# Window attention in a diffusion backbone: full-height low keys with zeros, masks added on VectorE with the row maximum, rotation by shifted multiplications

## Chip, cores and metric

One Trainium2 chip, of which the program uses one core. The metric is the device time of one execution in microseconds. The engines are named as in the profile: PE (TensorE matmul), PEld (its weight load), DVE (VectorE), ACT (ScalarE), POOL (GpSimd) and SP (SyncE, which here issues the DMAs).

## What is computed

A backbone of two layers runs over 256 context tokens and 256 latent tokens of width 1024. Layer 0 is feed-forward, DeltaNet, feed-forward; layer 1 is feed-forward, window attention, feed-forward. Of layer 1's attention only the latent outputs count. The part of the reference that matters here, cut down:

```python
q = _rms_norm(q.reshape(n_batch, n, SWA_HEADS, SWA_HEAD_DIM), q_gain)      # 16 heads of 64
k = _rms_norm(k.reshape(n_batch, n, SWA_KV_HEADS, SWA_HEAD_DIM), k_gain)   # 4 key heads
if rotate:                                       # latent tokens only
    q, k = _rope(q, cos, sin), _rope(k, cos, sin)
...
allowed = (jnp.abs(t_pos[:, None] - s_pos[None, :]) <= WINDOW) & (s_pos >= 0) & (s_pos < n_tok)
s_ctx = jnp.einsum('bqhgd,bkhd->bhgqk', qb, kc).astype(jnp.float32)
s_win = jnp.where(allowed, jnp.einsum('bqhgd,bkhd->bhgqk', qb, kb).astype(jnp.float32), -jnp.inf)
p = _sink_softmax(jnp.concatenate([s_ctx, s_win], axis=-1), sink_hg).astype(vb.dtype)
return (jnp.einsum('bhgqk,bkhd->bqhgd', p[..., :ctx_len], vc)
        + jnp.einsum('bhgqk,bkhd->bqhgd', p[..., ctx_len:], vb))
```

`_rope` splits the 64 features of a head in halves x1, x2 and gives x1 cos - x2 sin and x1 sin + x2 cos. The softmax has one more logit per head, the sink.

## The kernel before

Features lie on partitions: tokens are kept as 8 chunks of [128 features, 512 tokens], of which columns 0 to 255 are context (`CTX`) and 256 to 511 latent (`LAT`). Every product with a weight is made in three passes of a reduced fp32 format (fp32r): high times high, high times low, low times high (`mm3`). Weights are streamed from memory in tiles `raw` and `ub`; `_split` (L428) cuts them in high parts (a copy on ACT) and low parts (a subtraction, on DVE, or on POOL while `lo_pool` is set, as during the query projections). `w_ahead` (L458) keeps up to four units of 128 output columns split ahead of use. Working tiles [128, 512] come from a pool `u` of 76, PSUM tiles `mm` from its 8 banks. All other engines' instructions have the line L180 in the profile, matrix products L276, transposes L281, since a helper records them.

The order of work is set while the program is written out, by a class `Sched` (L65). It keeps a clock of TensorE work. Straight-line code advances it; background generators say how long they expect to wait (`self.at(...)`) and are resumed when the clock gets there. `note` (L93) estimates when an instruction of another engine ends from its engine and its width. So an instruction that is added, or dropped, moves the others in every engine's queue; each engine then works through its own queue in order.

The attention, `attention` (L1800), goes so:

- Its constants (`att_consts`, L1668) are loaded during the feed-forward block ahead of it: the rotation matrix `rotm`, a block matrix `blk64` for the norms, cosines and sines, the gains, the sinks, and `wmask`, [128, 384], made of three 128-column masks by ACT copies.
- Four units are projected first: two key units (two heads each) and two value units. Then the queries, eight pairs of heads `u`, one unit each.
- `att_qk` (L1691) works on a pair of heads. ACT squares, PE sums the squares over each head (`blk64`), ACT makes the inverse root with Ln and Exp, DVE multiplies by gain and root (`kn`). For latent tokens PE multiplies by `rotm` (L1706), which swaps the halves of a head and gives one the minus sign; DVE multiplies this product, in PSUM, by the sines; POOL multiplies `kn` by the cosines and adds. Then ACT copies the high parts and DVE subtracts for the low ones. A query tile holds the high part of one head in 64 partitions and its low part in the other 64; a key tile holds the high part twice; the keys' low parts of both heads share one tile.
- `att_worker` (L1740): four workers take 16 tasks, a pair of heads `u` by a tile of 128 latent queries `qt`. For each of the two heads, scores over 512 keys are three products into one PSUM bank: query (high and low) by high keys, 128 rows deep; identity by mask, 256 columns (L1755); high query by low keys, 64 rows deep (L1756). DVE takes the row maximum from PSUM (L1760), two small DVE operations bring in the sink, ACT makes the exponential from PSUM with the sum (L1767), DVE scales the rows, PE transposes them in four pieces, ACT copies, PE multiplies by the values, ACT and DVE write the high and low parts of the output.
- Behind the queries `begin` and `out_blocks` make the output projection, whose first products can stand among the attention's.

The lines of the scores before:

```python
rw = slice(64 * par, 64 * par + 64)
sc.append(self.cht())
self.mm(sc[par], q[par][:, qs], kh[par], stop=False)
self.mm(sc[par][:, LAT], self.identr, self.wmask[:, 128 - 128 * qt:384 - 128 * qt], start=False, stop=False)
self.mm(sc[par], q[par][rw, qs], kl[rw, :], start=False)
```

Of the kernel before, what the change touches and what calls it, by code (L numbers as in the profile page):

```python
# [22 lines left out]
def constants():  # L23
    """Arrays that depend on shapes alone."""
    c = {"ident": np.eye(128, dtype=np.float32)}
    # 128 rows: two chunks of 64 tokens; in variant e the half e runs forward and the other one backward
# [20 lines left out]
    d = np.arange(64)  # L47
    for b in (0, 64):
        at[b + 32 + np.arange(32), b + np.arange(32)] = -1.0
        at[b + np.arange(32), b + 32 + np.arange(32)] = 1.0  # L50
        at[b:b + 64, 128 + b:192 + b] = 1.0 / 64
# [8 lines left out]
    at[:, 768:1024] = np.sin(ang.astype(np.float64)).T[f]  # L60
    c["atc"] = at
    return c


class Sched:  # L65
    """Emission order: straight-line code advances a clock of TensorE work, and
    background generators are resumed when the clock reaches the time they asked for."""
# [9 lines left out]
    @staticmethod  # L77
    def cells(a):
        """a tile in parts of 64 partitions by 128 columns"""
        (ps, n), *rest = a.ap  # L80
        p, lo = divmod(a.offset, ps)
        hi = lo + sum((k - 1) * st for st, k in rest)
        return [(a.tensor.name, i, j) for i in range(p // 64, (p + n - 1) // 64 + 1)
                for j in range(lo // 128, hi // 128 + 1)]
# [8 lines left out]
    def note(self, eng, ins, outs, n, extra):  # L93
        """estimates when an instruction of another engine ends"""
# [14 lines left out]
    def product(self, ins, out, ns):  # L109
        """TensorE at the clock, other work first while the operands are awaited"""  # L110
# [59 lines left out]
class Queue:  # L170
    """an engine whose instructions are also noted in the schedule"""
# [38 lines left out]
class Kernel:  # L210
# [34 lines left out]
    def at(self, *aps):  # L245
        """time from now until these are expected"""
        return max(0.0, self.s.when(*aps) - self.s.clock)

# [35 lines left out]
    def mm3(self, ps, w, h, nk, sl=ALL, ks=None, start=True, stop=True):  # L284
        """ps[:, sl] = W^T h over nk chunks of 128, W and h in exact high and low parts."""
# [12 lines left out]
    def plan_weights(self):  # L298
        """Raw loads and the units of 128 output columns cut from them, in the order of use."""
# [4 lines left out]
        def raw(*parts):  # L304
            # outside of DeltaNet its tiles take loads as well
# [11 lines left out]
        def cols(mat, r0, nk, c0, w=256):  # L317
            """nk chunks of 128 rows from r0, w columns from c0 -> [128, nk, w]"""
# [91 lines left out]
    def _load(self, late=False):  # L410
        """loads into the raw tiles that are free, or soon (late = True: any that have no further use)"""
# [46 lines left out]
    def w_ahead(self):  # L458
        """splits the units to come once their loads are expected"""
# [29 lines left out]
    def setup(self):  # L489
# [18 lines left out]
        # tokens  # L508
# [6 lines left out]
        # modulation of the first norm and the first pairs of the first FFN, 128 features after the other  # L515
# [3 lines left out]
        # squares and transposes of the tokens  # L519
# [16 lines left out]
        # root mean squares of the tokens, from tokens on partitions to a row for every partition  # L536
# [12 lines left out]
    def setup_rows(self, rows):  # L549
        """vectors with their features on partitions"""  # L550
# [25 lines left out]
    def first_load(self, c):  # L576
        """weights of the first modulation and of the first pairs of the first FFN for 128 features"""
# [20 lines left out]
    def first_mod(self, c):  # L598
        """shift and scale of (layer 0, slot 0) for 128 features, and their norm"""
# [41 lines left out]
    def first_w(self, c):  # L641
        """high and low parts of the weights of 128 features"""
# [109 lines left out]
    def sq_block(self, d, sl, ps=None):  # L752
        """adds the squares of chunk d to the running sum"""
# [38 lines left out]
    def h_chunks(self, hf, l, slot, ks, pace=None):  # L792
        """high and low parts of the modulated norm of chunks ks, one group of tokens"""
# [70 lines left out]
    def mm_narrow(self, ps, w, sl):  # L864
        """W^T H for 32 columns in two parts: the high and the low part of W with the high part of H, and the high part
        and zeros with the low one"""
# [6 lines left out]
    def halves_first(self, n, evac, narrow=False):  # L873
        """the first n units, context tokens before latent ones"""
# [20 lines left out]
    def out_block(self, d, final):  # L895
        """the latent tokens of chunk d, tokens on partitions, to the output"""
# [15 lines left out]
    def out_blocks(self, h, nk, sl, l, v, nxt, final=None, begun=None):  # L912
        """X += gate * (W^T h); with nxt the squares of the sums and the next norm follow"""
# [77 lines left out]
    def start_pairs(self):  # L991
        """the first three pairs of the first FFN, chunk by chunk as the modulation arrives"""
# [19 lines left out]
    # Tokens of each segment are kept in the order of chunks 0, 3, 1, 2, so that 128 columns q hold the two chunks  # L1012
    # that the forward and the backward pass visit in the same step.
    # kinds of projection: 0 q, 1 k, 2 v, 3 z
# [38 lines left out]
    def dn_gates(self, ps):  # L1053
        """per-token gates from the projection in two parts of [32, 512], tokens on partitions, for both variants"""
# [58 lines left out]
    def dn_unit(self, kind, h, ps):  # L1113
        """evacuates the projection of head h: kind 0 q, 1 k, 2 v, 3 z"""
# [55 lines left out]
    def dn_ss(self, sq, g, dst):  # L1170
        """log of the sums of squares over the head dimension, tokens on partitions"""
# [14 lines left out]
    def dn_pairs(self, ps, lhs, rhs, g, qp):  # L1186
        """products over the head dimension inside each chunk, for two pairs of chunks and four heads"""
# [8 lines left out]
    def dn_prep(self, g):  # L1196
        """decays, the systems of each chunk and their inverses for the heads of group g"""
# [703 lines left out]
```

## Time and profile before

| | |
|---|---|
| runs | 1937.22, 1942.4 and 1944.46 us, median 1942.4 |
| profiled execution | span 1937.3 us; no time of its own beside the span is listed |
| busy in the span | PE 97%, PEld 81%, DVE 66%, ACT 49%, POOL 34% |
| first key norm on DVE | 1601.3 us |
| first row maximum | 1625.3 us |
| end of the last subtraction of the attention | 1714.7 us |
| row maxima, 32 | 21.0 us of DVE |
| mask products, 32 | 8.9 us of PE by the records |

How to read it: times in the trace are counted from the span's start. A group names output and inputs by the program's tiles without their numbers (`mm` is a PSUM bank, `u` a working tile, `st` a small tile of row statistics), then the shape. "Idle before" is the idle time of that engine right ahead of the instruction, with what ended it. Matmul records overlap by some ns, since their ends are modelled; how often one recurs says more than its length. PEclk is the granted TensorE clock as a share of full speed.

### The profile page before, as it was taken

The page shows a single profiled execution, that of the slowest core. Times are in us where ns is not written, and L with a number is a line of the kernel's source. Part 1 is how long each engine was busy: PE and PEld are TensorE (multiplying, and loading weights), DVE is VectorE, ACT ScalarE, POOL GpSimd, SP SyncE. Part 2 cuts the span into 40 slices and gives each one's busy share as a digit, 9 for nine tenths or more (in the row PEclk, how much of TensorE's full clock was granted, in tenths as well). Part 3 has the DMA queues.
Part 4 walks back from the last instruction along what each step waited for, and adds up shares of the span by engine and source line. Part 5 has one row for each costly group of instructions (what it writes and reads, how often), then busy time and mean ns, then how long its engine had stood idle before and what let it go on. Part 6 is the DMA issues. An engine that isn't in the chain of part 4 may idle for free.

```text
span 1937.3 us, 30131 instructions
## 1 busy us (share of the span) xinstructions
PE 1880.2 (97%) x11367; PEld 1560.9 (81%) x11367; DVE 1280.2 (66%) x2065; ACT 946.5 (49%) x2061; POOL 649.8 (34%) x597
## 2 busy tenths in 40 slices
PE   7999999989999999999999999999999999999999
PEld 5878788887776766887888888888888898689998
DVE  4897878855977966578888555643343356856565
ACT  4544544556476555464454344542222357755442
POOL 3344534454546435354445114320000057230000
PEclk8999999999999999999999999999999999999999
DMA  9655454413232152445645554433232334125552
GB/s 292 212 202 203 165 185 169 157 44 126 71 88 81 51 186 82 169 142 185 211 170 179 190 185 147 164 124 101 96 109 87 100 86 96 36 66 174 196 175 87
DMA packets 242376, 270.78 MB, mean 140 GB/s; under 512 B 11015, under 2 KB 198687, under 8 KB 242231
## 3 DMA queue, kind: packets, MB, share of 16 engines
q1 hardware_dynamic: 241943, 268.69, 42.4%
q8 instruction: 89, 1.46, 0.3%
q14 instruction: 56, 0.46, 0.1%
q0 software_dynamic: 144, 0.11, 0.0%
q10 hardware_dynamic: 144, 0.07, 0.0%
HBM read 258.34 MB, written 10.49 MB: 139 GB/s over the span
## 4 chain that ended last, share of the span: by engine, by line
PE 57%; DVE 6%; ACT 3%; issue 3%; POOL 1%; DMA 1%; POOLq 0%; DVEq 0%; ACTq 0%; SPq 0%
PE mm L276 56%; DVE u L180 5%; ACT u L180 3%; PE mm L281 1%; POOL u L180 1%; DVE st L180 1%; DVE big L180 0%; DMA u<-ZD 0%; DMA u<-XD 0%; DVE ub L180 0%; ACT L180 0%; POOLq L180 0%; DVEq L180 0%; ACT sc L180 0%; ACTq L180 0%
## 5 line engine op out<-in xcount | busy, mean ns | idle before, releaser
L276 PE MATMUL mm<-u 128*128 128x512 f32 (+6 forms) x10112 | 1798.5, 343 | 21.3 <-ACT u L180 9.6
L276 PEld LDWEIGHTS mm<-u 128*128 128x128 f32 (+2 forms) x10112 | 1491.4, 185 | 305.9 <-issue 54.4
L180 POOL TENSOR_TENSOR u<-u 128x512 f32<-128x512 f32 (+4 forms) x389 | 430.3, 1112 | 911.4 <-ACT u L180 868.3
L180 ACT ACTIVATE u<-u 128x256 f32<-128x256 f32 (+8 forms) x335 | 159.6, 488 | 488.1 <-DVE u L180 475.8
L180 ACT ACTIVATE u<-mm 128x512 f32<-128x512 f32 (+3 forms) x356 | 142.5, 414 | 283.1 <-PE mm L276 213.8
L180 DVE TENSOR_TENSOR u<-raw,u 128x512 fp32r<-128x512 f32 (+2 forms) x272 | 217.9, 845 | 27.3 <-ACT u L180 26.0
L180 DVE SCALAR_TENSOR_TENSOR u<-u,cc 128x512 f32<-128x512 f32 x196 | 229.3, 1170 | 3.9 <-DMA u<-in_ada_w 0.6
L180 DVE TENSOR_TENSOR u<-ub,u 128x512 fp32r<-128x512 f32 x254 | 199.8, 830 | 18.5 <-ACT u L180 17.3
L180 ACT ACTIVATE u<-raw 128x512 fp32r<-128x512 f32 (+1 forms) x374 | 205.8, 604 | 10.8 <-PE mm L276 5.7
L180 ACT ACTIVATE u<-u,cc 128x512 f32<-128x512 f32 x224 | 151.9, 711 | 82.5 <-DMA u<-in_ada_w 72.4
L180 DVE TENSOR_TENSOR u<-u,mm 128x512 f32<-128x512 f32 (+1 forms) x88 | 54.5, 619 | 206.5 <-PE mm L276 198.2
L180 POOL TENSOR_TENSOR u<-raw,u 128x512 fp32r<-128x512 f32 x98 | 130.4, 1354 | 135.7 <-ACT u L180 119.1
L180 ACT ACTIVATE u<-ub 128x512 fp32r<-128x512 f32 (+1 forms) x284 | 156.0, 605 | 10.2 <-DMA ub<-in_ffn_w 6.0
L180 DVE SCALAR_TENSOR_TENSOR u<-mm,mod,u 128x256 f32<-128x256 f32 x192 | 86.1, 478 | 106.4 <-PE mm L276 106.2
L180 DVE TENSOR_TENSOR u<-u 128x512 fp32r<-128x512 f32 (+5 forms) x125 | 82.6, 662 | 74.3 <-ACT u L180 72.5
L180 DVE SCALAR_TENSOR_TENSOR u<-u,mod 128x256 f32<-128x256 f32 (+1 forms) x140 | 88.8, 686 | 24.0 <-ACT u L180 23.7
L180 ACT ACTIVATE u<-u,mod 128x256 fp32r<-128x256 f32 (+1 forms) x124 | 56.2, 501 | 52.1 <-DVE u L180 51.7
L180 DVE SCALAR_TENSOR_TENSOR u<-mm,cw,u 128x510 f32<-128x510 f32 (+1 forms) x96 | 71.2, 743 | 8.1 <-ACT u L180 6.4
L281 PE MATMUL mm<-ident,u 128*128 128x128 f32 (+3 forms) x361 | 55.5, 283 | 11.3 <-DMA ident<-in_ident 4.4
L281 PEld LDWEIGHTS mm<-ident,u 128*128 128x128 f32 (+3 forms) x361 | 42.1, 145 | 23.5 <-ACT u L180 6.3
L276 PE MATMUL mm<-u,ones 128*32 128x512 f32 (+2 forms) x172 | 37.6, 551 | 14.5 <-DVE u L180 10.4
L180 POOL TENSOR_TENSOR u<-ub,u 128x512 fp32r<-128x512 f32 x30 | 41.5, 1406 | 22.1 <-ACT u L180 21.8
(118 smaller groups left out, 582.1 us busy)
## 6 DMA issues: line engine op xcount, KB each, us to landing
u<-in_ada_w SPq DMA_DIRECT2D x256, 256.0 KB, 5.6
ub<-in_ffn_w SPq DMA_DIRECT2D x59, 1024.0 KB, 5.1
raw<-in_ffn_w SPq DMA_DIRECT2D x57, 1024.0 KB, 5.1
raw<-in_dn_w_in SPq DMA_DIRECT2D x16, 1024.0 KB, 5.7
ub<-in_ada_w SPq DMA_DIRECT2D x12, 512.0 KB, 7.1
ub<-in_ffn_w SPq DMA_DIRECT2D x8, 768.0 KB, 4.6
raw<-in_ffn_w SPq DMA_DIRECT2D x8, 768.0 KB, 4.6
raw<-in_dn_w_out SPq DMA_DIRECT2D x4, 1024.0 KB, 6.2
```

Of the source, the lines that this page charges most:

```text
L180: r = f(*a, **k)
L276: self.nc.tensor.matmul(out, lhsT, rhs, start=start, stop=stop, **kw)
L281: self.nc.tensor.transpose(out, in_, self.ident[:k, :k])
```

## The change

Four edits, all in the attention of layer 1:

1. **Rotation.** The product with `rotm` and the one multiplication that reads it from PSUM go. Four multiplications of 32 partitions by 256 columns take their place: each reads 32 rows of `kn` and writes the product with the sines to the partner's 32 rows, three on DVE and one on POOL. The minus sign is now in the sines. POOL's multiplication by the cosines overwrites `kn`, so it follows all four.
2. **Low keys.** The low parts of the two heads of a key pair lie in two tiles instead of one. The other 64 partitions of each are filled with zeros by ACT (a copy with scale 0).
3. **Scores.** Two products, both 128 rows deep and 512 wide. The identity-by-mask product goes.
4. **Masks and maximum.** One DVE instruction reads the scores from PSUM and the mask from SBUF (`wmask` is now two [128, 512] tiles loaded from a new input), writes the sum to SBUF and accumulates its maximum. ACT's exponential then works in SBUF, in place.

Comments and docstrings are dropped as well. In the changed file the helpers' lines are L183 (engines), L279 (products) and L284 (transposes). The core of the diff:

```diff
-        at[b + 32 + np.arange(32), b + np.arange(32)] = -1.0
-        at[b + np.arange(32), b + 32 + np.arange(32)] = 1.0
...
-    at[:, 768:1024] = np.sin(ang.astype(np.float64)).T[f]
+    at[:, 768:1024] = np.sin(ang.astype(np.float64)).T[f] * np.where(p % 64 < 32, 1.0, -1.0)[:, None]
     c["atc"] = at
+    wm = np.zeros((128, 1024), np.float32)
+    wm[:, 384:512] = at[:, 256:384]
+    wm[:, 768:896] = at[:, 384:512]
+    c["wmc"] = wm
...
     def att_consts(self):
...
-        self.rotm, self.blk64 = t0[:, 0:128], t0[:, 128:256]
-        self.wmask = self.const([128, 384], "wmask", F32R)
+        self.blk64 = t0[:, 128:256]
+        self.wmask = [self.u(), self.u()]
+        for i in range(2):
+            nc.sync.dma_start(out=self.wmask[i], in_=a["wmc"][:, 512 * i:512 * i + 512])
...
-        for i, c0 in enumerate((384, 640, 256)):
-            if i == 1:
-                self.act(out=self.wmask[:, 128:256], in_=t0[:, 256:384], func=AF.Copy, scale=0.0)
-            else:
-                self.act(out=self.wmask[:, 128 * i:128 * i + 128], in_=t0[:, c0:c0 + 128], func=AF.Copy)
...
     def att_qk(self, ps, sl, gain, store, keys=False):
...
         nc.vector.scalar_tensor_tensor(out=kn[:, sl], in0=ps[:, sl], scalar=gain, in1=rs[:, sl], op0=ALU.mult, op1=ALU.mult)
         yield self.at(kn)
-        p2 = self.cht()
-        self.mm(p2[:, LAT], self.rotm, kn[:, LAT])
         t = self.u()
-        yield self.at(p2)
-        nc.vector.tensor_tensor(out=t[:, LAT], in0=p2[:, LAT], in1=self.sin, op=ALU.mult)
+        for i, b in enumerate((0, 64, 32, 96)):
+            o = b ^ 32
+            (nc.vector if i < 3 else nc.gpsimd).tensor_tensor(out=t[o:o + 32, LAT], in0=kn[b:b + 32, LAT],
+                                                              in1=self.sin[b:b + 32, :], op=ALU.mult)
+        yield self.at(t)
         nc.gpsimd.tensor_tensor(out=kn[:, LAT], in0=kn[:, LAT], in1=self.cos, op=ALU.mult)
         yield self.at(t)
         nc.gpsimd.tensor_tensor(out=kn[:, LAT], in0=kn[:, LAT], in1=t[:, LAT], op=ALU.add)
...
-        lo = self.u(dt=F32R) if keys else None
+        lo = [self.u(dt=F32R), self.u(dt=F32R)] if keys else None
         for par in range(2):
             for j in ((0, 1) if keys else (par,)):
                 self.act(out=st[par][half[j], sl], in_=kn[half[par], sl], func=AF.Copy)
+            if keys:
+                self.act(out=lo[par][half[1 - par], sl], in_=kn[half[1 - par], sl], func=AF.Copy, scale=0.0)
...
-            dst = lo[half[par], sl] if keys else st[par][half[1 - par], sl]
+            dst = lo[par][half[par], sl] if keys else st[par][half[1 - par], sl]
...
     def att_worker(self, todo):
...
-                rw = slice(64 * par, 64 * par + 64)
                 sc.append(self.cht())
                 self.mm(sc[par], q[par][:, qs], kh[par], stop=False)
-                self.mm(sc[par][:, LAT], self.identr, self.wmask[:, 128 - 128 * qt:384 - 128 * qt], start=False, stop=False)
-                self.mm(sc[par], q[par][rw, qs], kl[rw, :], start=False)
+                self.mm(sc[par], q[par][:, qs], kl[par], start=False)
...
-                nc.vector.tensor_reduce(out=st[:, 0, par:par + 1], in_=sc[par], axis=AX.X, op=ALU.max)
+                P.append(self.u())
+                nc.vector.tensor_tensor_reduce(out=P[par], in0=sc[par], in1=self.wmask[qt], scale=1.0, scalar=NEG,
+                                               op0=ALU.add, op1=ALU.max, accum_out=st[:, 0, par:par + 1])
...
-                P.append(self.u())
-                self.act(out=P[par], in_=sc[par], func=AF.Exp, bias=st[:, 1, par:par + 1],
+                self.act(out=P[par], in_=P[par], func=AF.Exp, bias=st[:, 1, par:par + 1],
                          accum_out=st[:, 2, par:par + 1])
```

The instructions of all engines stand in the same order as before up to the attention. In it they move. On PE, before, from the projection products ahead of the first scores on (`mm<-u 128x256` are products of projections, norms and rotations, `mm<-u 128x512` scores):

```order
L276 MATMUL mm<-u 128x256 x93
L276 MATMUL mm<-u 128x512
L276 MATMUL mm<-wmask,identr 128x256
L276 MATMUL mm<-u 128x512 x2
L276 MATMUL mm<-wmask,identr 128x256
L276 MATMUL mm<-u 128x512 x2
L276 MATMUL mm<-wmask,identr 128x256
L276 MATMUL mm<-u 128x512 x2
L276 MATMUL mm<-wmask,identr 128x256
L276 MATMUL mm<-u 128x512
L276 MATMUL mm<-u 128x256 x39
```

The same place after the change, where `mm<-ident,u` are transposes and `64x128` the products with the values:

```order
L279 MATMUL mm<-u 128x256 x192
L279 MATMUL mm<-u 128x512 x8
L284 MATMUL mm<-ident,u 128x128 x12
L279 MATMUL mm<-u 64x128 x8
L284 MATMUL mm<-ident,u 128x128 x4
L279 MATMUL mm<-u 128x512 x12
L279 MATMUL mm<-u 64x128 x8
```

All eight query projections now stand ahead of the first scores: counted from the key and value units on there are 368 products of 128x256 there instead of 278, 90 more.

On DVE before, from the second key norm to the first row maximum (`kg` and `qg` are the gains, so these are the norms of keys and queries; `64x512` and `64x256` are low parts):

```order
L180 SCALAR_TENSOR_TENSOR u<-mm,kg,u 128x512
L180 TENSOR_TENSOR u<-mm,u 128x256
L180 TENSOR_TENSOR u<-u 64x512 x4
L180 SCALAR_TENSOR_TENSOR u<-mm,qg,u 128x256
L180 TENSOR_TENSOR u<-mm,u 128x256
L180 SCALAR_TENSOR_TENSOR u<-mm,qg,u 128x256
L180 TENSOR_TENSOR u<-mm,u 128x256
L180 SCALAR_TENSOR_TENSOR u<-mm,qg,u 128x256
L180 TENSOR_TENSOR u<-u 64x256 x2
L180 TENSOR_TENSOR u<-mm,u 128x256
L180 TENSOR_REDUCE st<-mm 128x1 x2
```

On DVE after, the last part ahead of the first fused maximum, which is built as two instructions, `ISA u,st<-mm,u 128x512` and `ISA st 128x1`:

```order
L183 SCALAR_TENSOR_TENSOR u<-mm,qg,u 128x256
L183 TENSOR_TENSOR u<-u 32x256 x3
L183 SCALAR_TENSOR_TENSOR u<-mm,qg,u 128x256
L183 TENSOR_TENSOR u<-u 64x256 x2
L183 TENSOR_TENSOR u<-ub,u 128x512
L183 TENSOR_TENSOR u<-u 32x256 x3
L183 SCALAR_TENSOR_TENSOR u<-mm,qg,u 128x256
L183 ISA u,st<-mm,u 128x512
L183 ISA st 128x1
L183 ISA u,st<-mm,u 128x512
L183 ISA st 128x1
L183 SCALAR_TENSOR_TENSOR st<-st,nsink 128x2
```

The norms of all eight query pairs and the multiplications of seven stand ahead of the first maximum, where three norms stood; with the keys' there are 27 multiplications `32x256` ahead of it.

More of the change, by code (lines that the diff above doesn't have):

```diff
@@ L46, in constants @@
     at = np.zeros((128, 1024), np.float32)
-    d = np.arange(64)
     for b in (0, 64):
-        at[b + 32 + np.arange(32), b + np.arange(32)] = -1.0
-        at[b + np.arange(32), b + 32 + np.arange(32)] = 1.0
         at[b:b + 64, 128 + b:192 + b] = 1.0 / 64
```

## The prediction

> **What bounds the kernel now.** I read the page first, then busy time by stage, then the stage's own timeline, waits and groups.
>
> ```profile
> span 1937.3 us, 30131 instructions
> PE 1880.2 (97%) x11367; PEld 1560.9 (81%) x11367; DVE 1280.2 (66%) x2065; ACT 946.5 (49%) x2061; POOL 649.8 (34%) x597
> ```
>
> Over the span PE is the bound. But the change lies in the attention alone, so the stretches count: a feed-forward one for comparison, the attention from the first key norm on DVE to the first row maximum, and from there to its last subtraction.
>
> ```profile
> core 0: us, PE busy (x) PEld busy (x) DVE busy (x) ACT busy (x) POOL busy (x), PEclk, DMA share, GB/s
> 1400.00:1500.00 100.00, 100.00 (x443) 82.85 (x442) 35.55 (x62) 25.46 (x46) 0.00 (x0) 1.00 0.29 95
> 1601.30:1625.30 24.00, 23.72 (x175) 22.04 (x174) 11.64 (x17) 21.04 (x41) 21.52 (x19) 1.00 0.56 119
> 1625.30:1714.70 89.40, 84.61 (x630) 62.49 (x630) 66.36 (x170) 59.57 (x165) 21.52 (x23) 1.00 0.15 40
> 1600.00:1640.00 40.00, 38.83 (x260) 33.30 (x259) 25.53 (x45) 30.42 (x65) 30.46 (x28) 1.00 0.51 106
> ```
>
> PE is busy 95% of the last 89.4 us, yet DVE has 66.4 us of work there, and POOL is 76% busy in the 40 us from 1600 on. PE's waits in the attention (engine, operation, releaser: us, count, longest) are few:
>
> ```profile
> PE mm L276 <- ACT u L180: 5.4, 8, 2.1
> PE mm L281 <- DVE u L180: 2.2, 3, 1.0
> ```
>
> So PE binds by a margin of about 20 us over DVE. What is taken from PE can bring no more than that, and only if the scores start as early as now.
>
> **What leaves PE.** The PE timeline at the first scores, one rotation product, and the output projection behind the attention:
>
> ```profile
> 1624.50 0.28 PE L276 MATMUL mm<-wmask,identr 128*128 128x256 f32 x1
> 1624.71 0.92 PE L276 MATMUL mm<-u 64*128 64x512 f32 x2
> 1625.47 0.28 PE L276 MATMUL mm<-wmask,identr 128*128 128x256 f32 x1
> 1648.67 0.68 PE L276 MATMUL mm<-u 128*128 128x256 f32 x2
> 1714.46 18.46 PE L276 MATMUL mm<-u 128*128 128x256 f32 x150 [0.37 <-ACT u L180]
> ```
>
> A score recurs every 0.97 us (1624.50 to 1625.47): 0.21 for the mask, 0.76 for the 64-row product and the high one behind it. A full-height fp32r product of 256 columns takes 18.46/150 = 0.123 us, so I estimate twice that, 0.25 us, for 512 columns, two of them 0.49 us. Each of 32 scores saves 0.48 us, 15.4 us together. Ten rotations go, at most 0.68 us each: five of them behind the first scores, 3.4 us. The Trainium skill speaks against the padding: "TensorE: Matmul & The Clock Gate", section "Why this matters for your kernels", says that a product over 32 rows takes as long as one over 128. By it only the mask's 0.21 us a score would go, 6.7 us. The 0.76 us for two products, one of them of 64 rows, speaks otherwise here: two full-height ones would be 0.49.
>
> Also moved: all eight query projections now stand ahead of the first scores, 90 more products, 90 x 0.123 = 11.1 us. PE's work behind the first scores falls to 84.6 - 15.4 - 3.4 - 11.1 = 54.7 us, and the scores can't start before about 1625.3 + 11.1 - 3.4 (the five early rotations) = 1633 on PE's account.
>
> **What DVE and POOL get: the rotation.** Now it is one multiplication for each key or query pair with an operand in PSUM. The DVE timeline shows what that operand is worth while POOL is at work (its row is the last one, from POOL):
>
> ```profile
> 1601.30 0.75 DVE L180 SCALAR_TENSOR_TENSOR u<-mm,kg,u 128x512 f32<-128x512 f32 x1 [6.28 <-ACT u L180]
> 1622.44 2.47 DVE L180 TENSOR_TENSOR u<-u 64x256 fp32r<-64x256 f32 x2
> 1624.95 0.42 DVE L180 TENSOR_TENSOR u<-mm,u 128x256 f32<-128x256 f32 x1
> 1625.29 0.68 DVE L180 TENSOR_REDUCE st<-mm 128x1 f32<-128x512 f32 x1
> 1630.43 0.87 DVE L180 TENSOR_TENSOR u<-u 64x256 fp32r<-64x256 f32 x2
> 1621.91 2.73 POOL L180 TENSOR_TENSOR u<-raw,u 128x512 fp32r<-128x512 f32 x2
> ```
>
> Two subtractions with both operands in SBUF take 0.87 us where POOL rests (1630.43) and 2.47 us beside POOL's (1621.91 to 1624.64): 0.43 or 1.23 each. The multiplication that reads PSUM takes 0.42 in POOL's company. The new 32x256 multiplications have both operands in SBUF, so they join the kind that waits. This fits "SBUF — State Buffer" of the Trainium skill (section "SBUF: two separate sides"), by which DVE and POOL hold one pair of ports in turn.
>
> The rows for the rest of the sum, groups of 1598 to 1716 (busy us, mean ns of one | idle before):
>
> ```profile
> L180 DVE SCALAR_TENSOR_TENSOR u<-mm,kg,u 128x512 f32<-128x512 f32 x2 | 1.5, 751 | 6.8 <-ACT u L180 6.8
> L180 DVE SCALAR_TENSOR_TENSOR u<-mm,qg,u 128x256 f32<-128x256 f32 x8 | 3.9, 482 | 3.1 <-ACT u L180 3.0
> L180 DVE TENSOR_TENSOR u<-u 64x512 fp32r<-64x512 f32 x4 | 4.2, 1047 | 3.5 <-ACT u L180 3.3
> L180 DVE TENSOR_TENSOR u<-u 64x256 fp32r<-64x256 f32 x16 | 9.5, 596 | 1.9 <-ACT u L180 1.4
> L180 DVE TENSOR_TENSOR u<-ub,u 128x512 fp32r<-128x512 f32 x1 | 0.7, 693 | 1.1 <-ACT u L180 1.1
> L180 DVE TENSOR_TENSOR u<-mm,u 128x256 f32<-128x256 f32 x10 | 4.2, 422 | 6.9 <-PE mm L276 6.8
> L180 POOL TENSOR_TENSOR u<-u 128x256 f32<-128x256 f32 x20 | 16.1, 812 | 15.4 <-PE mm L276 12.5 <-DVE u L180 2.5
> L180 ACT ACTIVATE u<-u 64x512 fp32r<-64x512 f32 x8 | 5.0, 626 | 0.1
> L180 DVE TENSOR_REDUCE st<-mm 128x1 f32<-128x512 f32 x32 | 21.0, 683 | 2.0 <-PE mm L276 2.0
> ```
>
> In DVE's new order there stand, from the first key norm to the first fused maximum, 27 of the multiplications, two key norms, eight query norms, four key and two query low parts, and one weight low part. Without the multiplications: 2 x 0.751 + 8 x 0.482 + 4 x 1.047 + 2 x 0.596 + 0.693 = 11.4 us. DVE is idle 12.4 of the 24 us there now; most of that gets filled, and I leave 3 us, chosen between 0 and the 6.8 of the key norms' row. A multiplication costs between 0.43 and 1.23; by POOL's 76% I take 0.43 + 0.76 x 0.80 = 1.04, in all 28.1 us. First maximum: 1601.3 + 11.4 + 3 + 28.1 = **1643.8**, 18.5 us later than now. With 0.43 DVE would be there at 1627 and PE's 1633 decides; with 1.23 it is 1649.
>
> What queues behind: POOL's cosine multiplication must now wait for DVE's three, since it overwrites their source, and the weights' low parts stand behind it on POOL. POOL also gets ten multiplications, nine ahead of the first maximum, at 0.81 us each by its row (7.3 us), which would lift its share to 94% and a multiplication to 1.18 (+3.8 us, within the range). On ACT four more 64x512 copies, 2.5 us, stand ahead of the first query's norm; the waits of the key chain cover them, and they cost at most 2.5 us if DVE isn't late anyway.
>
> Costing nothing: three ACT copies of masks go and two 256 KB loads join those of the attention's other constants, beside feed-forward products that keep PE at 100%; uncovered, the loads would hold up a weight load by a few us.
>
> **The rest of the attention.** The maximum becomes a fused add and maximum, plus a second small instruction. Nearest rows: a two-operand pass over 128x512 with PSUM, an ACT read of an accumulator, and a tiny DVE operation. Then the DVE share of two stretches of 20 us:
>
> ```profile
> L180 DVE TENSOR_TENSOR u<-u,mm 128x512 f32<-128x512 f32 x66 | 45.2, 685 | 165.0 <-PE mm L276 156.7 <-ACT u L180 7.9
> L180 ACT ACTIVATION_READ_ACCUMULATOR u<-mm,st 128x1 f32 x32 | 6.7, 208 | 0.0
> 1672.24 0.15 DVE L180 TENSOR_TENSOR st<-st 128x2 f32<-128x2 f32 x1
> 1714.43 0.29 DVE L180 TENSOR_TENSOR u<-mm,u 128x128 fp32r<-128x128 f32 x1 [2.23 <-ACT u L180]
> 1620.00:1640.00 20.00, 19.12 (x111) 14.64 (x110) 17.59 (x34) 12.25 (x31) 13.47 (x14) 1.00 0.52 112
> 1660.00:1680.00 20.00, 17.80 (x131) 12.24 (x132) 16.87 (x46) 13.79 (x40) 2.85 (x3) 1.00 0.16 53
> ```
>
> The pass costs 0.685 against the reduction's 0.683; the second instruction I take at 0.15, 32 x 0.15 = 4.8 us, between 0 (fused for nothing) and 0.28 (0.21 like ACT's and a little more): 0 to 9 us. From DVE's 66.4 us go five query norms (2.4), five rotations (2.1) and the weight low part (0.7), now ahead of the first maximum: 61.2 + 4.8 = 66.0 us. That is over PE's 54.7 and ACT's 59.6, so DVE binds. A binding DVE through chains of six hand-overs fills, by the two rows, 88% and 84%; I take 86%: 66.0/0.86 = **76.7 us**, between 61.2/0.95 = 64 and 70/0.84 = 83. Now it is 1714.7 - 1625.3 = 89.4.
>
> The sum: 1643.8 + 76.7 = 1720.5, 5.8 us after 1714.7. PE also rests some 8 us between the last projection (about 1636) and the scores that wait for DVE. What a rest does to its clock shows right behind the attention:
>
> ```profile
> 1732.00:1736.00 4.00, 2.05 (x12) 1.25 (x10) 1.34 (x3) 1.36 (x4) 1.49 (x1) 0.99 0.29 87
> 1736.00:1740.00 4.00, 2.92 (x10) 2.39 (x11) 3.64 (x8) 3.18 (x7) 1.80 (x2) 0.50 0.52 177
> ```
>
> After 4 us half empty the granted clock is 0.50 for 4 us, so I add 2 us. Span 1937.3 + 7.8 = 1945.1. The page has no time of its own for this execution; the runs' median of 1942.4 is 5.1 above its span, so the forecast is **1950**. From its bounds (start 1639 to 1649, 71 to 83 us) its own range is about 1940 to 1962.
>
> **The rivals.**
> - *POOL is not in the way* (faster). The three multiplications of a pair meet POOL while it waits for them, take near 0.43, and PE's projections decide: first maximum by 1636, then 68 us (66/0.97) to 1704: 10.7 us earlier, **1932**. For it: POOL is in order and waits at the cosine for the very three. Against it: up to 23 weight parts stand among them. It decides if the first fused maximum comes before 1637. Chance 0.22.
> - *The padding doesn't do what it says.* A full-height product costs what the 64-row one does, 0.42, and a score 0.76. PE then has 54.7 + 32 x 0.27 = 63.3 us, still under DVE, but with fewer spare; 1.5 us for it gives **1952**. Against it is the 0.123 us of the projections. Chance 0.10.
> - *The clock* (slower). PE, 71% busy in small pieces, is granted half speed in three quarters of the rest: 54.7 x 1.75 = 95.7, by 95% 101 us instead of 76.7: 24 us on top, **1974**; it decides from half of it on (86 us, 1960). For it: the 0.50 row after one stretch at 51%. Against it: 1660 to 1680 shows 1.00 at 89% busy. The same Trainium skill page, section "Part 1: The HAM clock gate", has PE drop to half after an idle window of some 3.4 us and knows 4/8 and 8/8 alone; the 0.50 agrees. Chance 0.08.
>
> **How the numbers follow.** The forecast has 0.55, and 0.05 is left for what I don't see. About 0.5%, 9.7 us, is what a measurement of this kernel can tell from no change: 1932.7 to 1952.1. The forecast gives 0.30 within it and 0.25 above; the first rival 0.18 faster and 0.04 within; the second 0.05 and 0.05; the third 0.08 slower; the rest 0.02, 0.02 and 0.01. Faster 0.20, same 0.41, slower 0.39. Both signs hold much of it, so the range reaches to the first rival, 1930, and above to 1964, leaving out the lowest 64 us tail and most of the clock rival.
>
> **What would show it.** Right: first fused maximum at 1639 to 1649; 32x256 on DVE at about 1 us, long only beside POOL; DVE above 84% busy from there to the last subtraction, PE under 75%; scores of 0.49 us. Wrong: multiplications of 0.43 and a first maximum before 1637; a second instruction far from 0.15; granted clock of 0.5 through the stage; or a difference outside the attention, for which I have no term.

## The result and the profile after

The changed kernel takes 1952.07 us (median of 4 runs, 1950.98 to 1952.91), the kernel before 1940.56 beside it (4 runs): a ratio of 1.0059, 95% interval 1.0041 to 1.0076. That is 11.5 us more. The profiled execution spans 1949.8 us. One run of an experiment below, the new rotation with the old scores, took 8176 us; its row goes by the other three, which lie within 2.8 us.

The page of the changed kernel, its first two lines:

```profile
span 1949.8 us, 30141 instructions
PE 1869.1 (96%) x11315; PEld 1557.6 (80%) x11315; DVE 1300.6 (67%) x2117; ACT 949.6 (49%) x2062; POOL 660.9 (34%) x607
```

PE has 11 us less to do and DVE 20 us more. Where the time goes shows in stretches: from the first key norm on DVE to the first fused maximum (1601.5 to 1650.4), from there to the last subtraction (1726.7), and the latter in three parts.

```profile
core 0: us, PE busy (x) PEld busy (x) DVE busy (x) ACT busy (x) POOL busy (x), PEclk, DMA share, GB/s
1601.50:1650.40 48.90, 37.87 (x269) 34.53 (x268) 41.55 (x44) 32.47 (x67) 44.91 (x40) 0.90 0.51 108
1650.40:1726.70 76.30, 58.71 (x483) 47.83 (x483) 57.85 (x194) 51.86 (x142) 8.39 (x12) 0.84 0.05 15
1650.40:1665.00 14.60, 6.11 (x35) 5.09 (x36) 12.93 (x31) 7.97 (x21) 8.39 (x12) 0.52 0.22 74
1665.00:1682.00 17.00, 10.74 (x64) 8.29 (x63) 14.86 (x50) 12.04 (x34) 0.00 (x0) 0.70 0.00 0
1682.00:1726.70 44.70, 41.86 (x388) 34.45 (x386) 30.07 (x113) 31.84 (x89) 0.00 (x0) 1.00 0.01 1
```

The first stretch grew from 24.0 to 48.9 us; POOL is busy 92% of it and DVE 85%. The second shrank from 89.4 to 76.3. Together 25 us later and 13 us shorter: 12 us, nearly all of the 12.5 by which the spans differ. In the first 32 us after the first maximum DVE is at 88%, while PE rests half the time at a granted clock of 0.52 to 0.70; from 1682 on PE is at 94%.

DVE's timeline of the changed kernel, from the first key norm, and its largest groups of 1598 to 1735:

```profile
1601.53 0.75 DVE L183 SCALAR_TENSOR_TENSOR u<-mm,kg,u 128x512 f32<-128x512 f32 x1 [6.28 <-ACT u L183]
1602.31 3.27 DVE L183 TENSOR_TENSOR u<-u 32x256 f32<-32x256 f32 x3
...
1640.13 3.73 DVE L183 TENSOR_TENSOR u<-u 32x256 f32<-32x256 f32 x3
1643.89 0.48 DVE L183 SCALAR_TENSOR_TENSOR u<-mm,qg,u 128x256 f32<-128x256 f32 x1
1644.41 1.29 DVE L183 TENSOR_TENSOR u<-u 64x256 fp32r<-64x256 f32 x2
1645.73 1.11 DVE L183 TENSOR_TENSOR u<-ub,u 128x512 fp32r<-128x512 f32 x1
1646.87 3.11 DVE L183 TENSOR_TENSOR u<-u 32x256 f32<-32x256 f32 x3
1650.01 0.48 DVE L183 SCALAR_TENSOR_TENSOR u<-mm,qg,u 128x256 f32<-128x256 f32 x1
1650.41 0.68 DVE L183 CUSTOM_DVE_ANT_0 u<-mm,u 128x512 f32<-128x512 f32 x1
...
1654.71 2.57 DVE L183 TENSOR_TENSOR u<-u 32x256 f32<-32x256 f32 x3
```

```profile
L183 DVE TENSOR_TENSOR u<-u 32x256 f32<-32x256 f32 x30 | 33.0, 1099 | 1.1
L183 DVE CUSTOM_DVE_ANT_0 u<-mm,u 128x512 f32<-128x512 f32 x32 | 20.7, 685 | 5.0 <-PE mm L279 4.9
L183 DVE TENSOR_SCALAR u<-u,st 128x512 f32<-128x512 f32 x32 | 14.8, 505 | 0.6
L183 DVE TENSOR_TENSOR u<-u 64x256 fp32r<-64x256 f32 x16 | 7.1, 446 | 0.6
L183 DVE DVE_READ_ACCUMULATOR2_ANT st<- 128x1 f32 x32 | 2.6, 82 | 0.0
```

The three multiplications of a pair take 3.1 to 3.7 us in the lines ahead of the first maximum; the mean of all 30 is 1.10 each. The fused maximum (the group CUSTOM_DVE_ANT_0) takes 0.685, as the reduction did, and its second instruction 0.08. PE's waits in the changed kernel's attention:

```profile
PE mm L284 <- DVE u L183: 17.3, 3, 10.2
PE mm L279 <- DVE u L183: 7.5, 1, 7.5
```

What before was 2.2 us of waiting for DVE is 24.8 us now: PE has its projections done, and nothing else until DVE gets to the scores' operands and maxima.

### The profile page after: what moved, and what is told of

The parts are those of the page before. It is cut to its first block, busy times and chain, and to the rows that moved or that the text cites. A ratio compares the mean times of both kernels' runs of the same rounds, so it can differ in the third digit from the quotient of the medians.

```text
span 1949.8 us, 30141 instructions
## 1 busy us (share of the span) xinstructions
PE 1869.1 (96%) x11315; PEld 1557.6 (80%) x11315; DVE 1300.6 (67%) x2117; ACT 949.6 (49%) x2062; POOL 660.9 (34%) x607
## 4 chain that ended last, share of the span: by engine, by line
PE 56%; DVE 6%; ACT 4%; issue 3%; POOL 1%; DMA 1%; POOLq 0%; DVEq 0%; ACTq 0%; SPq 0%
PE mm L279 54%; DVE u L183 6%; ACT u L183 4%; PE mm L284 1%; POOL u L183 1%; DVE big L183 0%; DMA u<-ZD 0%; DMA u<-XD 0%; DVE st L183 0%; DVE ub L183 0%; ACT L183 0%; POOLq L183 0%; ACT st L183 0%; DVEq L183 0%; ACT sc L183 0%
## 5 line engine op out<-in xcount | busy, mean ns | idle before, releaser
L279 PE MATMUL mm<-u 128*128 128x512 f32 (+4 forms) x10092 | 1784.9, 342 | 30.4 <-DVE u L183 10.8
L279 PEld LDWEIGHTS mm<-u 128*128 128x128 f32 (+1 forms) x10092 | 1489.2, 185 | 305.5 <-issue 43.3
L183 POOL TENSOR_TENSOR u<-u 128x512 f32<-128x512 f32 (+5 forms) x399 | 439.3, 1108 | 896.4 <-ACT u L183 859.5
L183 ACT ACTIVATE u<-u 128x512 fp32r<-128x512 f32 (+8 forms) x339 | 162.2, 490 | 493.4 <-DVE u L183 474.9
L183 ACT ACTIVATE u<-mm 128x128 f32<-128x128 f32 (+3 forms) x356 | 142.7, 414 | 277.1 <-PE mm L279 205.6
L183 DVE TENSOR_TENSOR u<-raw,u 128x512 fp32r<-128x512 f32 (+2 forms) x272 | 216.6, 840 | 27.8 <-ACT u L183 26.7
L183 DVE SCALAR_TENSOR_TENSOR u<-u,cc 128x512 f32<-128x512 f32 x196 | 228.0, 1163 | 4.2 <-DMA u<-in_ada_w 0.9
L183 DVE TENSOR_TENSOR u<-ub,u 128x512 fp32r<-128x512 f32 x254 | 200.7, 833 | 17.4 <-ACT u L183 16.1
L183 ACT ACTIVATE u<-raw 128x512 fp32r<-128x512 f32 (+1 forms) x374 | 205.8, 604 | 10.0 <-DMA raw<-in_ffn_w 7.0
L183 DVE TENSOR_TENSOR u<-u,mm 128x512 f32<-128x512 f32 (+1 forms) x88 | 54.5, 619 | 208.2 <-PE mm L279 199.9
L183 ACT ACTIVATE u<-u,cc 128x512 f32<-128x512 f32 x224 | 151.7, 711 | 82.5 <-DMA u<-in_ada_w 66.5
L183 POOL TENSOR_TENSOR u<-raw,u 128x512 fp32r<-128x512 f32 x98 | 131.9, 1369 | 167.3 <-ACT u L183 153.8
L183 DVE TENSOR_TENSOR u<-u 128x512 fp32r<-128x512 f32 (+6 forms) x155 | 112.5, 726 | 74.7 <-ACT u L183 71.7
L183 ACT ACTIVATE u<-ub 128x512 fp32r<-128x512 f32 (+1 forms) x284 | 156.0, 605 | 10.1 <-DMA ub<-in_ffn_w 5.9
L183 DVE SCALAR_TENSOR_TENSOR u<-mm,mod,u 128x256 f32<-128x256 f32 x192 | 86.1, 477 | 107.1 <-PE mm L279 106.8
L183 DVE SCALAR_TENSOR_TENSOR u<-u,mod 128x256 f32<-128x256 f32 (+1 forms) x140 | 88.8, 685 | 23.9 <-ACT u L183 23.6
L284 PE MATMUL mm<-ident,u 128*128 128x128 f32 (+3 forms) x361 | 59.7, 299 | 27.2 <-DVE u L183 18.3
L183 ACT ACTIVATE u<-u,mod 128x256 fp32r<-128x256 f32 (+1 forms) x124 | 56.2, 501 | 52.3 <-DVE u L183 51.9
L284 PEld LDWEIGHTS mm<-ident,u 128*128 128x128 f32 (+3 forms) x361 | 45.6, 154 | 41.0 <-DVE u L183 19.1
L183 DVE SCALAR_TENSOR_TENSOR u<-mm,cw,u 128x510 f32<-128x510 f32 (+1 forms) x96 | 71.1, 742 | 8.1 <-ACT u L183 6.4
L279 PE MATMUL mm<-u,ones 128*32 128x512 f32 (+2 forms) x172 | 37.3, 548 | 13.4 <-DVE u L183 9.3
L183 DVE SCALAR_TENSOR_TENSOR u<-u,aS,mm 128x128 f32<-128x128 f32 x96 | 31.2, 344 | 22.1 <-PE mm L279 21.5
```

Source lines behind the costliest of these rows:

```text
L183: r = f(*a, **k)
L279: self.nc.tensor.matmul(out, lhsT, rhs, start=start, stop=stop, **kw)
L284: self.nc.tensor.transpose(out, in_, self.ident[:k, :k])
```

## The experiments

Theory 1 is that of the prediction: the multiplications wait beside POOL and make the scores late. Theory 2 is the moved order, theory 3 the clock behind PE's rest; theories 4 (POOL's load) and 5 (DVE's bare work) came up on the way. The experiments were run in three groups, beside which the kernel before took 1940.72, 1942.07 and 1940.9 us; so a difference of two kernels out of different groups is uncertain by a good microsecond, and the ratios are the safer guide. Attentions start up to 6 us apart in profiled executions of different kernels, so lengths below count from the first key norm: to the first maximum ("start"), and from there to the output projection's run of products ("rest"). Before: 24.0 and 89.2 us. Changed: 48.9 and 76.0.

| kernel | us | ratio to before, 95% interval | start | rest |
|---|---|---|---|---|
| changed | 1952.07 | 1.0059 (1.0041 to 1.0076) | 48.9 | 76.0 |
| sines in PSUM | 1943.83 | 1.0015 (1.0006 to 1.0024) | 40.0 | 77.1 |
| matrix rotation, new scores | 1930.86 | 0.9942 (0.9928 to 0.9955) | 29.3 | 73.6 |
| new rotation, old scores | 1953.34 | 1.0060 (1.0045 to 1.0075) | 42.1 | 83.0 |
| PE kept warm | 1951.85 | 1.0059 (1.0045 to 1.0074) | 49.1 | 75.5 |
| early order | 1947.44 | 1.0031 (1.0019 to 1.0043) | 37.5 | 80.5 |
| early order, sines in PSUM | 1945.12 | 1.0014 (1.0006 to 1.0023) | 31.0 | 85.9 |
| low product of 64 rows, matrix rotation | 1935.23 | 0.9963 (0.9951 to 0.9975) | 29.3 | 79.2 |
| four on DVE, sines in PSUM | 1934.47 | 0.9972 (0.9961 to 0.9983) | 36.5 | 71.3 |
| four on DVE | 1946.32 | 1.0026 (1.0011 to 1.0041) | 47.4 | 70.5 |
| four on DVE, sines in PSUM, early order | 1939.99 | 0.9994 (0.9984 to 1.0004) | 31.3 | 81.8 |

**The sines in PSUM.** One operand of DVE's three multiplications is moved to a PSUM bank; every engine's order stays that of the changed kernel, but for the one copy.

```diff
-                                                              in1=self.sin[b:b + 32, :], op=ALU.mult)
+                                                              in1=(self.sinp[b:b + 32, LAT] if i < 3 else self.sin[b:b + 32, :]), op=ALU.mult)
...
+        self.sinp = self.mmt()
+        self.act(out=self.sinp[:, LAT], in_=self.sin, func=AF.Copy)
         self.halves_first(4, first)
```

> The changed kernel with one operand moved: the sines that DVE's three rotation multiplications read lie in a PSUM bank (one ACT copy more, one bank less); every engine's order is otherwise that of the changed kernel. Theory 1, the two-SBUF-operand multiplications wait beside POOL: they fall from 1.10 to about 0.42 us each, 27 of them are 18 us shorter, the first fused maximum comes at 1636 to 1641 instead of 1650.4 and the time is 1932 to 1940. Theory 2, the moved order (all eight query projections ahead of the first scores) is what delays the scores: the multiplications may get shorter, the first maximum stays at 1646 or later and the time within 3 us of 1952.

The multiplications with their sines in PSUM, as a group:

```profile
L183 DVE TENSOR_TENSOR u<-u,mm 32x256 f32<-32x256 f32 x30 | 12.4, 414 | 1.1
```

From 1.10 to 0.41 us each, by an operand's place alone. The time falls by 8.2 us, 1952.07 to 1943.83. The first maximum comes at 1642.3, not at 1636 to 1641, and the kernel is still behind the one before: theory 1's mechanism is shown, but it is not all of the loss.

**The parts of the change apart.** First the matrix rotation of before with the new keys, scores and masks; then the new rotation alone in the kernel before.

```diff
-        t = self.u()
-        for i, b in enumerate((0, 64, 32, 96)):
...
+        p2 = self.cht()
+        self.mm(p2[:, LAT], self.rotm, kn[:, LAT])
+        t = self.u()
+        yield self.at(p2)
+        nc.vector.tensor_tensor(out=t[:, LAT], in0=p2[:, LAT], in1=self.sin, op=ALU.mult)
```

> The changed kernel with the rotation of before (product with the rotation matrix, one multiplication from PSUM); padded keys and masks on DVE stay. Theory 1: no late multiplications, first fused maximum at 1630 to 1638, time 1928 to 1937, faster than before. Theory 2 (order): 1945 or more, as long as projections stand ahead of the scores. If the score part is itself worth nothing (DVE binds anyway): 1939 to 1944.

The second has the same lines the other way round, with the signs in the sines:

> The kernel before with the rotation by shifted multiplications alone; scores, masks and maxima as before. Theory 1: multiplications near 1.1 us, first row maximum at 1643 to 1651, then PE has about 75 to 80 us of work left: last subtraction at 1720 to 1730, time 1948 to 1958, clearly slower than before. If the lateness comes from the score part instead: 1938 to 1945.

Scores and masks alone make the kernel faster, 1930.86 us, 9.9 under the 1940.72 beside it; the rotation alone makes it slower, 1953.34, 12.6 over. Both times lie inside what theory 1 expected. In the full change the rotation costs 1952.07 - 1930.86 = 21 us: with it in place the new scores bring 1.3 us (1953.34 to 1952.07) instead of 9.9. These 21 us include the order, since with the matrix rotation only five projections stand ahead of the first scores again. The windows of the kernel with the matrix rotation:

```profile
1640.00:1660.00 20.00, 15.88 (x121) 12.79 (x123) 19.16 (x55) 15.50 (x40) 6.81 (x8) 0.91 0.27 89
1660.00:1680.00 20.00, 18.09 (x169) 14.11 (x167) 19.02 (x70) 17.09 (x51) 0.73 (x1) 1.00 0.01 2
1680.00:1700.00 20.00, 20.00 (x198) 17.51 (x194) 14.37 (x54) 15.14 (x43) 0.00 (x0) 1.00 0.01 2
```

DVE is at 95% for 40 us, then PE at 100%: here the rest, 73.6 us, is really bound, by one and then by the other.

**PE kept warm.** 112 products that nobody reads fill PE's two longest rests.

```diff
+            self.warm({0: 56}.get(2 * u + qt, 0), kh)
             for par in range(2):
...
+            self.warm({1: 56}.get(2 * u + qt, 0), kh)
             ns = self.nsink[:, 8 * c + u % 4:8 * c + u % 4 + 5:4]
```

> The changed kernel with 112 more products on PE that nobody reads, 56 ahead of the first scores and 56 behind the first four scores, where PE rested 7.5 and 10.2 us. Theory 3, the half clock is what the rest costs: granted clock back to about 1.00 from 1640 on, scores and transposes at full rate, time 1943 to 1948. Theory 1, DVE is late and sets the pace there: clock up, but the time falls by at most 3 us, 1949 to 1952.

The same 20 us of the changed kernel, then of this one:

```profile
1640.00:1660.00 20.00, 4.91 (x13) 3.28 (x14) 19.29 (x33) 4.78 (x14) 18.32 (x22) 0.52 0.32 105
```

```profile
1640.00:1660.00 20.00, 13.84 (x105) 12.76 (x104) 19.32 (x32) 4.77 (x14) 18.90 (x22) 0.95 0.33 105
```

The granted clock rises from 0.52 to 0.95 there, and the time stays: 1951.85. DVE has 19.3 us of work in both. The half clock is real and costs nothing in these 20 us, because PE waits for DVE. (Between 1660 and 1680 it is 0.67 and 0.76, so the clock wasn't tried through the whole stage.)

**The order.** The multiplications count for nothing in the schedule's clock, so the first eight score products are written out with 41 products still behind them, all but one of projections.

```diff
+        free = dict(self.s.free)
         for i, b in enumerate((0, 64, 32, 96)):
...
-        yield self.at(t)
+        self.s.free.update(free)
+        self.s.mark(t[:, LAT], self.s.clock + 400.0)
```

> The changed kernel, but the four multiplications of a pair count for nothing in the schedule's clock and the cosine multiplication is written out with them, so the order comes out nearly as with the rotation by matrix: five projections' products instead of eight ahead of the first scores, the rest between. Multiplications as in the changed kernel (both operands in SBUF). If the order is what costs most: first fused maximum at 1632 to 1638, time 1936 to 1942. If the waiting beside POOL costs most: multiplications still near 1.1 us, first maximum at 1640 to 1646, time 1945 to 1950.

> The same early order, and the sines of DVE's multiplications in PSUM. If lateness comes from these two alone (long multiplications, projections ahead): first fused maximum at 1628 to 1634 and time 1929 to 1936, equal to the kernel with the matrix rotation within 4 us. If the bare work of three multiplications for one on DVE, 8 us more, is what costs: 1936 to 1941.

With SBUF operands the early order takes 4.6 us off the changed kernel, and the start comes to 37.5 us; 1947.44 and a first maximum at 1641.9 are what was expected if the waiting beside POOL costs most. With the sines in PSUM it takes nothing off (1945.12 after 1943.83), though the start is 31.0 us, almost that of the matrix rotation: the rest grows to 85.9. What was won at the start is lost behind it, where PE now waits in the middle, in the early kernel with sines in PSUM:

```profile
1643.46 7.63 PE L279 MATMUL mm<-u 128*128 128x256 f32 x30 [6.18 <-ACT u L183]
...
1655.29 1.72 PE L284 MATMUL mm<-ident,u 128*128 128x128 f32 x8 [4.20 <-DVE u L183]
...
1668.16 2.45 PE L279 MATMUL mm<-u 128*64 128x128 f32 x16 [6.42 <-ACT u L183]
```

Of the 30 products the first 20 are 128x256 ones that now stand between scores; PE waits 6 us for their operands, and the next eight score products queue behind. So the order delays the start (40.0 to 31.0 us), but theory 2 falls as the cause of the time: 1945.12 lies above both times expected, 1929 to 1936 and 1936 to 1941, and the 13 us that were left (1943.83 to 1930.86) did not go with the order. The move of the sines is worth less here, 2.3 us (1947.44 to 1945.12), than the 8.2 us in the order of the changed kernel. POOL's timeline, its last low parts of query weights (`ub`), first in that kernel, whose key norm comes at 1603.80, then with the matrix rotation, where it comes at 1599.05:

```profile
1647.78 2.54 POOL L183 TENSOR_TENSOR u<-ub,u 128x512 fp32r<-128x512 f32 x2
```

```profile
1637.90 2.69 POOL L185 TENSOR_TENSOR u<-ub,u 128x512 fp32r<-128x512 f32 x2 [0.41 <-ACT u L185]
```

This pair ends 46.5 us after the key norm in the one and 41.5 in the other. That led to theory 4.

**POOL's load.** All four multiplications on DVE, with the sines in PSUM or in SBUF. Both have one order, with 11 products of the last projection behind the first scores.

```diff
-            (nc.vector if i < 3 else nc.gpsimd).tensor_tensor(out=t[o:o + 32, LAT], in0=kn[b:b + 32, LAT],
+            nc.vector.tensor_tensor(out=t[o:o + 32, LAT], in0=kn[b:b + 32, LAT],
```

> The changed kernel with all four multiplications on DVE and their sines in PSUM: POOL has ten multiplications fewer (7.7 us). Theory 4, POOL's queue is the rest of the loss (weight low parts late, PE's projections and the cosines behind them): POOL's last low part of a query weight ends by 1643, first fused maximum at 1632 to 1637, time 1931 to 1937. Theory 5, the bare work of more multiplications on DVE is the rest: ten more, 4 us, on DVE, time 1944 to 1948.

> The changed kernel with all four multiplications on DVE, both operands in SBUF; the same order as with the sines in PSUM. Theory 4 alone (POOL's load, waiting beside POOL is secondary): below 1945. Theory 1 (each SBUF multiplication waits beside POOL's instructions): 9 more waiting multiplications ahead of the first maximum, but POOL done sooner: multiplications at 0.8 to 1.1 us, first maximum at 1646 to 1652, time 1946 to 1955.

> All four multiplications on DVE, sines in PSUM, and the early order; POOL's order is that of the kernel with the matrix rotation. Theory 4: first fused maximum at 1629 to 1633, no wait of several us for a projection's weights, time 1929 to 1935, equal to the matrix rotation (1930.9) within 4 us. Theory 5 (DVE's bare work, 40 multiplications of 0.41 for 10): 1939 to 1945.

The groups with the sines in PSUM, then in SBUF:

```profile
L183 DVE TENSOR_TENSOR u<-u,mm 32x256 f32<-32x256 f32 x40 | 16.7, 417 | 1.1
```

```profile
L183 DVE TENSOR_TENSOR u<-u 32x256 f32<-32x256 f32 x40 | 33.0, 825 | 1.1
```

With the sines in PSUM the kernel takes 1934.47 and the first maximum comes at 1635.6, both inside what theory 4 expected. That is 9.4 us less than with three multiplications on DVE, but the order changed along with POOL's load. And the weights' low parts were not late there: POOL's last pair for the queries ends 40.6 us after the key norm with three on DVE and 40.4 with four. So the 9.4 us are load and order together, by a way that this pair doesn't show.

With the operands in SBUF it is 1946.32, above the 1945 that theory 4 alone allowed and inside what theory 1 expected: the four on DVE are worth 5.8 us there and the place of the sines 11.9. This kernel also shows what its multiplications wait for. Two of its groups of four on DVE, then POOL's instructions around the second:

```profile
1634.76 4.66 DVE L183 TENSOR_TENSOR u<-u 32x256 f32<-32x256 f32 x4
1650.64 1.70 DVE L183 TENSOR_TENSOR u<-u 32x256 f32<-32x256 f32 x4
```

```profile
1648.78 1.83 POOL L183 TENSOR_TENSOR u<-u 128x256 f32<-128x256 f32 x2 [0.36 <-DVE u L183]
1656.45 1.28 POOL L183 TENSOR_TENSOR u<-ub,u 128x512 fp32r<-128x512 f32 x1 [5.84 <-ACT u L183]
```

Of the 40 multiplications 14 ran with no POOL instruction beside them, and each took 0.41 to 0.42 us with both operands in SBUF. The other 26 took 1.04 on the mean.

The early order on top, with the sines in PSUM, makes the kernel slower again, 1939.99, with a start of 31.3 and a rest of 81.8 us, where theory 4 expected 1929 to 1935 and no wait of several us on PE; two of 6.8 us remain. An earlier first maximum is worth nothing by itself. Why exactly the early order lengthens the rest by 10 us stays open: the waits weren't removed one by one.

POOL's load at an unchanged order shows in this last kernel beside the early one with three on DVE. Both have the same order on every engine, but for the ten multiplications. Taking them off POOL brings 5.1 us (1945.12 to 1939.99; 4.0 by the kernels before beside them), though DVE does them instead, and POOL's last pair of low parts ends 41.4 instead of 46.5 us after the key norm. So theory 4 is shown for 4 to 5 us in this order, and theory 5 as sole cause of the rest falls.

A path from the changed kernel to the matrix rotation adds up to the 21 us: the place of the sines 8.2, POOL's ten multiplications with the order that comes with them 9.4, and 3.6 left, in which DVE still does 40 multiplications of 0.42 us instead of ten and the order moves once more. It is one path and no division into causes, since the move of the sines is worth 2.3 us in one kernel and 11.9 in another.

**The padding alone.** The kernel with the matrix rotation, with the low product on its 64 rows again.

```diff
-                self.mm(sc[par], q[par][:, qs], kl[par], start=False)
+                rw = slice(64 * par, 64 * par + 64)
+                self.mm(sc[par], q[par][rw, qs], kl[par][rw, :], start=False)
```

> The kernel with padded keys, masks on DVE and the rotation by matrix (1930.9), with the low product over its 64 rows again; the zeros are still written. If padding makes the product cheaper as the rows suggest, a score is 0.2 us longer on PE; DVE is busy 19 of 20 us in the stage's middle, so the time rises by 0 to 4 us only: 1931 to 1935. If PE binds in this kernel: 6 us more, 1937. If a 64-row product costs the same: 1931, and scores recur as fast.

PE's rows in the part where it does not wait, a task of two scores and their products with the values each: first with 64 rows, then padded.

```profile
1676.69 2.79 PE L281 MATMUL mm<-u 128*128 128x512 f32 x20
1680.26 2.79 PE L281 MATMUL mm<-u 128*128 128x512 f32 x20
```

```profile
1672.61 2.21 PE L281 MATMUL mm<-u 128*128 128x512 f32 x20
1675.60 2.19 PE L281 MATMUL mm<-u 128*128 128x512 f32 x20
```

A task recurs every 3.57 us with 64-row products and every 2.99 us padded: 0.29 us a score. The time is 1935.23 against 1930.86, 4.4 us more (3.0 by the kernels before beside them); 0.2 us a score and 1931 to 1935 were expected. So of the 9.9 us of the score part the padding brings 3 to 4 and the masks on DVE about 6.

## Why the prediction was right, point by point

- **Direction and size.** Forecast 1950, 7.8 us over the kernel before; measured 1952.07, 11.5 over. The way there held: a later start, a shorter rest, nothing outside the attention (12.0 us later at the output projection, spans 12.5 apart).
- **The start.** Forecast first maximum at 1643.8, measured 1650.4, which is outside its own bounds of 1639 to 1649. The mechanism was right and the size too small. The 27 multiplications ahead of the first maximum take 33.0 - 2.57 = 30.4 us (all 30 less the three at 1654.71), 2.3 more than said, 1.13 each for 1.04. The 3 us left for DVE's idle time were short by more: 48.90 - 41.55 = 7.4 us are idle, 6.0 of them ahead of the keys' low parts and the first two query norms, where DVE waits for ACT. The fixed part, 41.55 - 30.4 = 11.1 us, was as forecast (11.4). The prediction had written down the share of 94% for POOL and priced it, 3.8 us, but took 76%.
- **Two SBUF operands wait, one in PSUM doesn't.** Shown by the sines in PSUM, 0.41 for 1.10 us, and by the 14 multiplications without POOL beside them, 0.41 to 0.42 with both operands in SBUF. This agrees with the Trainium skill, "SBUF — State Buffer", section "SBUF: two separate sides", where one instruction of DVE with two SBUF inputs or one of POOL holds the pair of ports.
- **The rest.** Forecast 76.7, measured 76.3, but partly by chance. The terms were wrong: DVE's work is 57.9 us, not 66.0, though the sum had left out the three multiplications behind the first maximum (2.5 us). The second instruction costs 0.08, not 0.15. And DVE's other instructions got shorter in this stretch: the three small operations on the row statistics 9.1 us for 12.3 before, the scaling of the rows 14.8 for 16.9, the 64x256 subtractions 5.9 for 7.1. POOL is busy 8.4 us of it for 21.5 before, which would explain that; it wasn't tested. DVE doesn't bind all of it either: it is at 88% for 32 us, then PE at 94%. The sentence that DVE would be above 84% and PE under 75% throughout was wrong (76% and 77%). The prediction's own range of the time took 71 us as the lower end of the rest, where its working had 64; with 64 it would have begun about 7 us lower.
- **The clock.** The clock falls, as said, but the term of 2 us for it isn't borne out: keeping PE warm from 1640 to 1660 changed nothing. Whether the 0.67 behind that costs anything wasn't tried. The rival with the clock needed a rest of 86 us or more and falls with 76.3. The Trainium skill, "TensorE: Matmul & The Clock Gate", section "Part 1: The HAM clock gate", gives half rate after an idle window, and the 0.52 over the 20 us with PE's longest rests agrees. In these 20 us it had no price.
- **POOL is not in the way.** This rival falls in its own words: POOL was 92% busy in the start. What it named as the point of decision, a first maximum before 1637, was reached in five experiments, and two of these were not faster than before (1945.12 and 1939.99). The prediction had no term for POOL's own ten multiplications beyond what they do to DVE's; at an unchanged order they are worth 4 to 5 us.
- **The padding.** Of the 0.48 us a score that the prediction took off PE, 0.27 were for the padding (0.76 to 0.49). The experiment shows 0.29. By the Trainium skill, "TensorE: Matmul & The Clock Gate", section "Why this matters for your kernels", a product over 32 rows takes as long as one over 128. Here one over 64 rows, between full-height ones, takes longer, and the measurement decides.
- **Span and median.** The 5.1 us between the span and the median before are 2.3 after, so 2.8 us of luck lie in the sum: by spans the forecast was 1945.1 and the measurement 1949.8.

## What to carry to other kernels

When work moves from one engine to another, ask first where the operands lie: an instruction with one operand in PSUM ran at 0.41 us beside a busy POOL and took 1.10 with both in SBUF, and the same edit with the sines in PSUM and POOL's ten multiplications on DVE turns a loss of 11.5 us into a gain of 6.4. Test the parts of a change apart: here a gain of 9.9 us was buried under a rotation that cost 21. The kernel with the matrix rotation, 1930.86 us, beats both. Test a step at an unchanged order where you can, for what it is worth depends on what else waits: moving the sines brought 8.2, 2.3 and 11.9 us in three kernels. An earlier start of the scores is no gain by itself, when what is pulled ahead of it or pushed behind it then waits in the middle.

## What the runs showed of the hardware

A product on 64 rows between full-height ones is dear on PE, and so is its neighbour. From one record's start to the next, a full-height product of 512 columns takes 0.235 us ahead of another one (median of the 27 between 1660 and 1700 us, matrix rotation with padding). With the low product on 64 rows it takes 0.43 us (median of 32), and so does the 64-row product behind it (median of 32). Half the rows thus cost nearly twice, and the neighbour pays as well. What a row of 64-row products alone would take, no run shows.

A multiplication of 32 partitions is no cheaper than one of 128: on DVE, with one operand in PSUM, 32x256 took 0.414 us and 128x256 0.422 in the kernel before. Cut in four, a multiplication costs four times as much. The last surprise is the second half of the fused maximum: reading DVE's accumulator takes 0.08 us, where ACT's takes 0.21.
